# Skipped gather rows and a new place for three pieces of work in the expert stream of a two-block network

## The chip, the cores and the metric

The kernel runs on one core of a Trainium2 chip. The metric is the device time of one execution in microseconds (us). The kernel before takes 3088.03 us, the median of 3 runs (3087.74 to 3088.43).

In this text TensorE (PE) does matrix products, and PEld is its loading of stationary operands; VectorE (DVE) and ScalarE (ACT) do elementwise work, GpSimd (POOL) some elementwise work and the indirect transfers, and SyncE (SP) issues the plain DMA transfers.

## The reference, cut to what matters

The reference applies one block of attention and gated delta-rule layers and then a second block of two layers, each with a mixer, a mixture of experts and a gate. The change concerns the mixture of experts alone, which comes twice. 512 tokens of width 1024 each choose 2 of 32 experts; an expert is a gated product of width 512:

```python
def expert_block(args):
    idx, e = args
    xb = x_pad[idx]
    hb = jax.nn.silu(xb @ w_gate[e]) * (xb @ w_up[e])
    return hb @ w_down[e]
```

All inputs are float32. The two results of a token are weighted by the router's softmax and added to the residual.

## The kernel before, in words

**Routing (`route`, from L1330).** For each layer TensorE computes the router's logits, and VectorE finds the two experts of each token and the rank of each token within its expert. A one-hot product on TensorE then gives `mps`, for each slot of each expert (64 slots per expert) the number of its entry plus one, and zero where the slot is empty. `tokens` (L1470) turns this into token numbers for the gather, an empty slot becoming token 0, and `slots` (L1477) into destinations for the scatter, an empty slot becoming a number far out of range, which the scatter's bounds check leaves out. `rows` (L1483) writes the normalized tokens to a table in HBM through two SBUF buffers `xg`. Tokens beyond 64 for one expert would go through a loop of extra passes (`overflow`); in the traced execution it makes no pass.

**Gather (`gather`, L1504).** One indirect DMA on POOL brings 128 rows of 4 KB, the slots of a pair of experts, into `xg`. Later TensorE transposes them (L1519, 8 products), ScalarE and VectorE split the result into a high and a low float32r part `pk` (L425, L426), and ScalarE copies the last quarter unsplit into `xf` (L1525). The high and low part of 64 tokens stand side by side as one stationary operand of 128 columns.

**Expert stream (`experts`, L1716).** The weights of an expert come as six tiles of 1 MB. They are used in 11 units, named `(e, k, part)`: gate (k = 0, 1), up (k = 2, 3) and down (k = 4, 5). For each unit ScalarE makes the high part of a weight slice (L425, tile `wh` or `X`) and VectorE the low part by subtraction (L426, `wl` or `X`). TensorE multiplies both with `pk` (`inner`, L1562; `outer` for the down product, L1588). To save splitting work, one slice in eight of gate and up, and a quarter of down, is not split: it is multiplied as plain float32 (`also`, L1570 with `xf`, L1599 in the down product). The splits run 6 units ahead of the products (`AHEAD`), and the code of a step stands in the order split, products, further work. `pin` fixes this order on TensorE, VectorE and ScalarE: each engine executes its instructions as they are written.

The further work of a step, in the kernel before:

- at `(e, 0, 1)` `middle(e - 1)` (L1573): TensorE folds the two halves of gate and up of the expert before (L1580), ScalarE takes `tanh` (L1583), VectorE multiplies twice (L1584, L1585, tile `mth`), and ScalarE and VectorE split the result into `hk`;
- at `(e, 1, 1)` and `(e, 3, 1)` ScalarE copies the finished gate or up accumulator to SBUF (L1752), which frees it;
- at `(e, 2, 1)` of every odd expert but the last the transposes and the `pk` split of the next pair;
- after the down products `finish` (L1603) adds the halves (L1609, L1610) and scatters the rows (L1611).

There are three accumulators `acc`, taken in the order gate, up, and the two halves of the down product of the expert before. So the gate of an expert takes the buffer of the up product of the expert before it. The weight tiles have six buffers, `wh`, `wl` and `X` four each.

Of the kernel before, what the change touches and what calls it, by code (L numbers as in the profile page):

```python
# [13 lines left out]
I32 = mybir.dt.int32  # L14
# [3 lines left out]
OP = mybir.AluOpType  # L18
AX = mybir.AxisListType

P = 128
D = 1024
# [12 lines left out]
N_EXP, D_EXP = 32, 512  # L35
BLK = 64
# [143 lines left out]
class Net:  # L180
# [1142 lines left out]
    def route(self, i):  # L1323

        nc, a = self.nc, self.a
        v, act, pe = nc.vector, nc.scalar, nc.tensor
        X, rstd, gx = self.x_in
        ps = self.acc()[:72]
# [11 lines left out]
        table = self.rows(i, gx, rstd)  # L1340
# [41 lines left out]
        for c in range(NC):  # L1382
# [4 lines left out]
                               op0=OP.add, op1=OP.mult)  # L1387
# [16 lines left out]
        mps = self.aux()[:, 0:32]  # L1404
        for k in range(2):
# [3 lines left out]
            for c in range(NC):  # L1409
                pe.matmul(mps, R[:, c].rearrange("p b s -> p (b s)"), idk[:, k, c], start=(k + c == 0),  # L1410
                          stop=(k == 1 and c == NC - 1))
        tk = self.t([P, N_EXP // 2], "tk", 1, I32)
        tk2 = self.t([P, N_EXP], "tk2", 1, I32)
        self.tokens(tk2, mps)
        for b in range(2):
            v.tensor_copy(tk[b * BLK:(b + 1) * BLK], tk2[b * BLK:(b + 1) * BLK, b::2])
        mp = self.t([BLK, N_EXP], "mp", 1, I32)
        self.slots(mp, mps[:BLK])

        def weights():  # L1420

# [22 lines left out]
        def further():  # L1444
# [20 lines left out]
            v.tensor_copy(more[:, 0:1], nst[:, 31:32])  # L1465
            v.tensor_scalar(more[:, 1:], bx, float(N_EXP - 1), None, op0=OP.min)
            return place, more
        return table, tk, mp, further, weights

    def tokens(self, tk, ps):  # L1470

        v = self.nc.vector
        v.tensor_scalar(tk, ps, -1.0, 0.0, op0=OP.add, op1=OP.max)
        v.tensor_scalar(tk, tk, 1, None, op0=OP.logical_shift_right)

    def slots(self, mp, ps):

        v = self.nc.vector
        em = self.t([BLK, N_EXP], "em", 1)[:, :ps.shape[1]]
        v.tensor_scalar(em, ps, 0.0, float(1 << 20), op0=OP.is_equal, op1=OP.mult)  # L1480
        v.scalar_tensor_tensor(mp, ps, -1.0, em, op0=OP.add, op1=OP.add)

# [18 lines left out]
            self.nc.tensor.transpose(tp[:, j * P:(j + 1) * P], x(j)[:, c * P:(c + 1) * P], self.ident)  # L1501
        return tp

    def gather(self, table, idx, m):  # L1504

        nc = self.nc
        v, act, pe = nc.vector, nc.scalar, nc.tensor
        xg = self.t([P, D], "xg", 2)
        nc.gpsimd.indirect_dma_start(out=xg[:m], out_offset=None, in_=table[:, :],  # L1509
                                     in_offset=bass.IndirectOffsetOnAxis(ap=idx, axis=0),  # L1510
                                     bounds_check=S - 1, oob_is_err=False)
        yield
        n = m // BLK
        pk = self.t([P, KT, n, P], "pk", 2, FR)
        xf = self.t([P, n, BLK], "xf", 2)
        for half in range(2):
            tp = self.aux()
            for k in range(4):
                pe.transpose(tp[:, k * m:(k + 1) * m], xg[:m, (4 * half + k) * P:(4 * half + k + 1) * P],  # L1519
                             self.ident[:m, :m])  # L1520
            tv = tp[:, 0:4 * m].rearrange("p (k e t) -> p k e t", k=4, e=n)
            o = pk[:, 4 * half:4 * half + 4]
            self.split(o[:, :, :, 0:BLK], o[:, :, :, BLK:P], tv)
            if half:
                act.activation(xf, tv[:, 3], AF.Copy)  # L1525
        yield [(pk[:, :, e], xf[:, e]) for e in range(n)]
# [36 lines left out]
    def inner(self, ps, x, k, h, l, also):  # L1563

        pe = self.nc.tensor
        pk, xf = x
        for q in range(h.shape[1]):
            pe.matmul(ps, pk[:, k + q], h[:, q], start=(k + q == 0), stop=False)  # L1568
            if also is not None:
                pe.matmul(ps[0:BLK], xf, also, start=False, stop=False, skip_group_check=True)  # L1570
            pe.matmul(ps, pk[:, k + q], l[:, q], start=False, stop=also is not None)  # L1571

    def middle(self, gu):  # L1573

# [55 lines left out]
    def moe(self, i, xs, nxt):  # L1630
        nc, a = self.nc, self.a
        v, act, pe = nc.vector, nc.scalar, nc.tensor
        self.compute = [nc.tensor.engine, nc.vector.engine, nc.scalar.engine]
        ym = self.dram.tile([N_SLOT, D], F32, name=f"ym{i}", tag=f"ym{i}", bufs=1)
        table, tk, mp, further, weights = self.route(i)
        pair = lambda q: self.gather(table, tk[:, q:q + 1], P)
        g = pair(0)
        next(g)
        place, more = further()
# [8 lines left out]
        with self.tc.For_i(0, extra, 1) as b:  # L1648
            eo = nc.sync.value_load(more[0:1, bass.ds(b + 1, 1)], min_val=0, max_val=N_EXP - 1)
            sl = self.t([P, BLK], "sl", 1)  # L1650
            v.tensor_scalar(sl, self.slot1, cb, None, op0=OP.add)
            v.tensor_scalar(cb, cb, float(BLK), None, op0=OP.add)
            bc = lambda x: x.unsqueeze(1).to_broadcast([P, NC, BLK])
            mps = self.aux()[:BLK, 0:1]
            for k in range(2):
                sk = self.t([P, S], "bc", 3).rearrange("p (c s) -> p c s", c=2 * NC)[:, 0:NC]
                v.tensor_tensor(sk, place[:, k * NC:(k + 1) * NC].unsqueeze(2).to_broadcast([P, NC, BLK]), bc(sl),
                                op=OP.is_equal)
                for c in range(NC):
                    pe.matmul(mps, sk[:, c], self.ids[:, k * NC + c:k * NC + c + 1], start=(k + c == 0),  # L1660
                              stop=(k == 1 and c == NC - 1))
            mc, tc = self.t([BLK, 1], "mc", 1, I32), self.t([BLK, 1], "tc", 1, I32)
            self.slots(mc, mps)
            self.tokens(tc, mps)
            go = self.gather(table, tc, BLK)
            next(go)
            self.overflow(i, eo, next(go)[0], mc, ym)
        self.tc.no_sync_barrier()
# [45 lines left out]
    def experts(self, i, ws, xs2, pair, mp, ym, weights):  # L1714
# [3 lines left out]
        nc = self.nc  # L1718
# [10 lines left out]
        for n in range(len(units) + AHEAD):  # L1729
# [13 lines left out]
            if k < 4:  # L1743
                if (k, part) == (0, 0) and e % 2 == 0 and e + 2 < N_EXP:
                    g = pair(e // 2 + 1)
                    next(g)
                if (k % 2, part) == (0, 0):
                    acc[e] = self.acc()
                self.inner(acc[e], xs2[e // 2][e % 2], 4 * (k % 2) + 2 * part, *ready.popleft())
                if (k % 2, part) == (1, 1):  # L1750
                    gu.setdefault(e, []).append(self.tmp())
                    act.activation(gu[e][-1], acc[e], AF.Copy)  # L1752
                if (k, part) == (0, 1) and e:
                    hid[e - 1] = self.middle(gu.pop(e - 1))
                if (k, part) == (2, 1) and e % 2 and e + 1 < N_EXP:
                    xs2.append(next(g))
                if (e, k, part) == (2, 2, 0):
                    wt = weights()
            else:
                r = k % 2 * 2 + part  # L1760
                if e == N_EXP - 1 and r == 0:
                    hid[e] = self.middle(gu.pop(e))
                if r == 0:
                    acc[e, "y"] = [self.acc() for _ in range(2)]
                self.outer(acc[e, "y"], hid[e], r, *ready.popleft())
                if r == 2:
                    self.apart(self.finish(acc.pop((e, "y")), self.tmp, mp[:, e:e + 1], ym), e)
# [177 lines left out]
```

## Time and profile before

| | |
|---|---|
| median of 3 runs | 3088.03 us |
| the profiled execution | 3087.97 us |
| its span | 3086.2 us |
| TensorE busy, whole span | 2896.1 us (94%) |
| weight loads (PEld) | 2175.4 us (70%) |
| VectorE busy | 2466.1 us (80%) |
| ScalarE busy | 1755.4 us (57%) |
| GpSimd busy | 467.6 us (15%) |
| bytes moved by DMA | 599.29 MB |

The two expert streams are where the DMA engines are busiest: the page's 40 slices show 395 to 413 GB/s there, and below 160 GB/s in nearly all of the first half of the span. The first stream lies at about 1592 to 2124 us, the second at about 2447 to 2980 us. In a timeline row the columns are the start in us, the duration in us, the engine, the line, the operation, the tile written and those read, the shapes, and the number of instructions merged into the row; idle time of the engine before it, and what ended it, stand in brackets. Since instructions of one engine overlap by about 0.1 us, the time that one takes from its queue is the distance to the next start.

### The profile page before, as it was taken

How to read it: one execution, taken by the hardware profiler on the slowest of the kernel's cores; microseconds unless marked ns; L12 is line 12 of the kernel's file. 1: busy time of each engine (PE TensorE's matmuls, PEld its weight loads, DVE VectorE, ACT ScalarE, POOL GpSimd, SP SyncE). 2: the span in 40 equal slices, each digit the busy share in tenths (PEclk: the TensorE clock that was granted, in tenths of full speed). 3: DMA queues.
4: the chain of work that ended last, by engine and by line, in shares of the span. 5: the costliest groups of instructions: out<-in, count | busy, mean ns of one | idle time of the engine just before them, and what ended most of it. 6: DMA issues, size and time to landing. Idle time of an engine off the chain costs nothing.

```text
span 3086.2 us, 39076 instructions
## 1 busy us (share of the span) xinstructions
PE 2896.1 (94%) x13517; PEld 2175.4 (70%) x13517; DVE 2466.1 (80%) x4540; ACT 1755.4 (57%) x2953; POOL 467.6 (15%) x457
## 2 busy tenths in 40 slices
PE   8998999999999999999979999999997799999997
PEld 6687878886778778878855666665775566666656
DVE  7899787867998578855558888887889588888876
ACT  3554443544444333542357777876476477877864
POOL 1111110011121010020011111111122111111112
PEclk9999999999999999999989999999999899999998
DMA  5221221242211222232249999997223399999981
GB/s 159 79 62 53 72 83 62 82 127 94 75 55 62 73 78 76 90 106 79 96 195 395 413 405 401 409 397 293 65 82 113 143 394 408 411 411 404 401 305 59
DMA packets 248663, 599.29 MB, mean 194 GB/s; under 512 B 29212, under 2 KB 159726, under 8 KB 215694
## 3 DMA queue, kind: packets, MB, share of 16 engines
q1 hardware_dynamic: 237582, 567.38, 49.0%
q0 software_dynamic: 10880, 29.37, 2.7%
q8 instruction: 108, 1.77, 0.2%
q14 instruction: 93, 0.76, 0.1%
HBM read 573.60 MB, written 31.49 MB: 196 GB/s over the span
## 4 chain that ended last, share of the span: by engine, by line
PE 39%; issue 33%; DVE 16%; POOL 7%; ACT 3%; DMA 2%; POOLq 0%; SPq 0%; ACTq 0%; DVEq 0%
PE acc L521 10%; PE acc L522 10%; PE acc L520 10%; POOL ym L1611 4%; DVE wl L426 2%; DVE tmp L953 2%; PE aux L432 1%; PE aux L1111 1%; PE aux L1106 1%; POOL xg L1509 1%; PE aux L463 1%; PE aux L843 1%; DMA xg<-xr,tk 1%; DVE sel L674 1%; PE aux L828 1%
## 5 line engine op out<-in xcount | busy, mean ns | idle before, releaser
L425 ACT ACTIVATE wh<-w 128x1024 fp32r<-128x1024 f32 (+1 forms) x592 | 577.8, 1003 | 377.7 <-PE acc L521 336.2
L426 DVE TENSOR_TENSOR wl<-w,wh 128x1024 fp32r<-128x1024 f32 (+1 forms) x592 | 672.7, 1161 | 67.0 <-ACT wh L425 61.1
L520 PE MATMUL acc<-X,wh 128*128 128x512 f32 (+1 forms) x1504 | 607.4, 404 | 18.1 <-DVE tmp L898 7.0
L521 PE MATMUL acc<-X,wh 128*128 128x512 f32 (+1 forms) x1536 | 616.5, 401 | 0.3 <-DVE X L426 0.3
L522 PE MATMUL acc<-X,wl 128*128 128x512 f32 (+1 forms) x1504 | 602.0, 401 | 5.3 <-DVE wl L426 5.3
L426 DVE TENSOR_TENSOR X<-w,X 128x1024 fp32r<-128x1024 f32 (+1 forms) x352 | 380.8, 1122 | 62.7 <-ACT X L425 62.1
L425 ACT ACTIVATE X<-w 128x1024 fp32r<-128x1024 f32 (+1 forms) x352 | 326.6, 971 | 33.4 <-DMA w<-in_w_exp_gate_dram 10.7
L520 PEld LDWEIGHTS acc<-X,wh 128*128 128x128 f32 (+1 forms) x1504 | 285.5, 190 | 81.5 <-DVE tmp L898 7.4
L521 PEld LDWEIGHTS acc<-X,wh 128*128 128x128 f32 (+1 forms) x1536 | 292.0, 190 | 58.3 <-DVE X L426 1.1
L522 PEld LDWEIGHTS acc<-X,wl 128*128 128x128 f32 (+1 forms) x1504 | 285.2, 190 | 67.0 <-DVE wl L426 8.0
L1611 POOL DMA_INDIRECT ym<-yb,mp x64 | 136.6, 2134 | 807.6 <-DVE yb L1610 807.6
L1568 PE MATMUL acc<-X,pk 128*128 128x512 f32 x448 | 185.8, 415 | 20.1 <-ACT tmp L1752 14.5
L1568 PE MATMUL acc<-wh,pk 128*128 128x512 f32 x448 | 181.5, 405 | 11.6 <-ACT tmp L1752 11.6
L1571 PE MATMUL acc<-X,pk 128*128 128x512 f32 x448 | 185.9, 415 | 0.0
L1571 PE MATMUL acc<-wl,pk 128*128 128x512 f32 x448 | 183.0, 408 | 0.0
L1570 PE MATMUL acc<-w,xf 128*64 128x512 f32 x256 | 137.5, 619 | 0.0
L1571 PEld LDWEIGHTS acc<-X,pk 128*128 128x128 f32 x448 | 86.3, 193 | 66.4 <-DVE X L426 17.9
L1571 PEld LDWEIGHTS acc<-wl,pk 128*128 128x128 f32 x448 | 84.2, 188 | 65.8 <-issue 18.7
L1580 PEld LDWEIGHTS aux<-fold,tmp 128*128 128x128 f32 x1024 | 124.7, 192 | 8.1 <-ACT tmp L1752 2.7
L479 POOL TENSOR_TENSOR tmp<-tmp,tmp 128x512 f32<-128x512 f32 x60 | 86.1, 1440 | 279.8 <-ACT tmp L472 236.2
L1580 PE MATMUL aux<-fold,tmp 128*128 128x64 f32 x1024 | 122.0, 272 | 2.5 <-ACT tmp L1752 2.5
L1599 PE MATMUL acc<-w,mth 128*64 128x512 f32 x256 | 123.8, 606 | 0.0
(558 smaller groups left out, 5364.8 us busy)
## 6 DMA issues: line engine op xcount, KB each, us to landing
w<-in_w_exp_gate_dram SPq DMA_DIRECT2D x128, 1024.0 KB, 7.9
w<-in_w_exp_up_dram SPq DMA_DIRECT2D x128, 1024.0 KB, 7.8
w<-in_w_exp_down_dram SPq DMA_DIRECT2D x128, 1024.0 KB, 8.1
w<-in_w_in_dram SPq DMA_DIRECT2D x72, 1024.0 KB, 5.0
w<-in_w_in_a_dram SPq DMA_DIRECT2D x12, 1024.0 KB, 4.9
w<-in_w_out_dram SPq DMA_DIRECT2D x8, 1024.0 KB, 4.9
w<-in_w_ple_gate_dram SPq DMA_DIRECT2D x8, 1024.0 KB, 12.0
X<-ym SPq DMA_DIRECT2D x16, 512.0 KB, 5.6
```

Source lines behind the costliest of these rows:

```text
L425: self.nc.scalar.activation(h, x, AF.Copy)
L426: self.nc.vector.tensor_sub(l, x, h.bitcast(F32))
L479: nc.gpsimd.tensor_add(t, tot[0], sq)
L520: mm(ps, wh[:, k], xh[k], start=(k == 0), stop=False)
L521: mm(ps, wh[:, k], xl[k], start=False, stop=False)
L522: mm(ps, wl[:, k], xh[k], start=False, stop=(k == kt - 1))
L1568: pe.matmul(ps, pk[:, k + q], h[:, q], start=(k + q == 0), stop=False)
L1570: pe.matmul(ps[0:BLK], xf, also, start=False, stop=False, skip_group_check=True)
L1571: pe.matmul(ps, pk[:, k + q], l[:, q], start=False, stop=also is not None)
L1580: pe.matmul(fp[:, (4 * q + f) * BLK:(4 * q + f + 1) * BLK], gu[q][:, f * P:(f + 1) * P], self.fold, start=True, stop=True)
L1599: pe.matmul(pss[c][0:BLK], hv[:, 3], also[:, c], start=False, stop=False, skip_group_check=True)
L1611: return nc.gpsimd.indirect_dma_start(out=ym[:, :], out_offset=bass.IndirectOffsetOnAxis(ap=mp, axis=0), in_=y, in_offset=None, bounds_che ...
```

## The change: what it does

1. Empty slots are left out of the gather. `tokens` now shifts the scatter's numbers right by one, so an empty slot's token number is far out of range too, and the bounds check of the indirect DMA leaves its row out. Since such rows keep what was in the buffer, the two buffers `xg` are now taken once per layer and set to zero by POOL before the first gather.
2. In `inner` the unsplit product stands last in its unit, behind the products with the high and with the low part; before, it stood between them.
3. `middle(e - 1)` moves from `(e, 0, 1)` to `(e, 1, 1)`, and the transposes of the next pair from `(e, 2, 1)` to `(e, 3, 1)`. Both stand right behind the unit's products and ahead of the copy of the accumulator.

The core of the diff:

```diff
+        mp = self.t([P, N_EXP], "mp", 1, I32)
         tk2 = self.t([P, N_EXP], "tk2", 1, I32)
-        self.tokens(tk2, mps)
+        self.slots(mp, mps)
+        self.tokens(tk2, mp)
...
-        mp = self.t([BLK, N_EXP], "mp", 1, I32)
-        self.slots(mp, mps[:BLK])
...
+    def tokens(self, tk, mp):
+        self.nc.vector.tensor_scalar(tk, mp, 1, None, op0=OP.logical_shift_right)
...
-    def tokens(self, tk, ps):
-        v = self.nc.vector
-        v.tensor_scalar(tk, ps, -1.0, 0.0, op0=OP.add, op1=OP.max)
-        v.tensor_scalar(tk, tk, 1, None, op0=OP.logical_shift_right)
...
             pe.matmul(ps, pk[:, k + q], h[:, q], start=(k + q == 0), stop=False)
-            if also is not None:
-                pe.matmul(ps[0:BLK], xf, also, start=False, stop=False, skip_group_check=True)
             pe.matmul(ps, pk[:, k + q], l[:, q], start=False, stop=also is not None)
+        if also is not None:
+            pe.matmul(ps[0:BLK], xf, also, start=False, stop=True, skip_group_check=True)
...
-        pair = lambda q: self.gather(table, tk[:, q:q + 1], P)
+        xg = [self.t([P, D], "xg", 2) for _ in range(2)]
+        for x in xg:
+            nc.gpsimd.memset(x, 0.0)
+        pair = lambda q: self.gather(table, tk[:, q:q + 1], P, xg[q % 2])
...
+                if (k, part) == (1, 1) and e:
+                    hid[e - 1] = self.middle(gu.pop(e - 1))
+                if (k, part) == (3, 1) and e % 2 and e + 1 < N_EXP:
+                    xs2.append(next(g))
                 if (k % 2, part) == (1, 1):
                     gu.setdefault(e, []).append(self.tmp())
                     act.activation(gu[e][-1], acc[e], AF.Copy)
-                if (k, part) == (0, 1) and e:
-                    hid[e - 1] = self.middle(gu.pop(e - 1))
-                if (k, part) == (2, 1) and e % 2 and e + 1 < N_EXP:
-                    xs2.append(next(g))
```

The first place is ScalarE's queue around `hk` and the gate copy of an odd expert in the first stream. `wh` and `X` of 128x1024 are whole weight splits, those of 128x512 half ones; `mth` is the `tanh`, `hk` ScalarE's half of the hidden split, and the row `tmp<-acc` is the gate copy. Before:

```order
L425 ACTIVATE wh_16271<-w_16260 128x512
L1583 ACTIVATE mth_16288<-aux_16279 128x256
L425 ACTIVATE hk_16292<-mth_16288 128x4x64
L425 ACTIVATE wh_16297<-w_16295 128x1024
L425 ACTIVATE wh_16305<-w_16295 128x1024
L1752 ACTIVATE tmp_16312<-acc_16266 128x512
L425 ACTIVATE X_16316<-w_16314 128x1024
```

After the change, in the same place:

```order
L425 ACTIVATE wh_16265<-w_16254 128x512
L425 ACTIVATE wh_16275<-w_16273 128x1024
L425 ACTIVATE wh_16283<-w_16273 128x1024
L1580 ACTIVATE mth_16299<-aux_16290 128x256
L425 ACTIVATE hk_16303<-mth_16299 128x4x64
L1756 ACTIVATE tmp_16306<-acc_16260 128x512
L425 ACTIVATE X_16310<-w_16308 128x1024
```

Two whole splits that stood behind `hk` now stand ahead of `tanh`, and the gate copy stands between `hk` and the next split.

The second place is the same queue a little later, around the `pk` pieces, `xf` and the up copy (again `tmp<-acc`). Before:

```order
L425 ACTIVATE pk_16333<-aux_16335 128x8x64
L425 ACTIVATE pk_16333<-aux_16342 128x8x64
L1525 ACTIVATE xf_16334<-aux_16342 128x128
L425 ACTIVATE X_16350<-w_16324 128x1024
L425 ACTIVATE X_16359<-w_16357 128x1024
L1752 ACTIVATE tmp_16365<-acc_16319 128x512
L425 ACTIVATE wh_16367<-w_16357 128x512
L425 ACTIVATE wh_16379<-w_16377 128x1024
```

After:

```order
L425 ACTIVATE X_16327<-w_16318 128x1024
L425 ACTIVATE X_16336<-w_16334 128x1024
L425 ACTIVATE pk_16342<-aux_16344 128x8x64
L425 ACTIVATE pk_16342<-aux_16351 128x8x64
L1522 ACTIVATE xf_16343<-aux_16351 128x128
L1756 ACTIVATE tmp_16359<-acc_16313 128x512
L425 ACTIVATE wh_16361<-w_16334 128x512
L425 ACTIVATE wh_16373<-w_16371 128x1024
```

The two whole splits that followed `xf` now precede the `pk` pieces, and the up copy follows `xf` at once, with the half split behind it.

The third place is POOL's queue at the start of a stream, as a difference: four table writes from `xg`, then the first gather.

```order
-L1494 DMA xr_14322<-xg_14365 128x1024
-L1509 DMA xg_14468<-xr_14322,tk_14458 128x1024
-L1647 TENSOR_LOAD rt_3195_14498
+L1492 DMA xr_14322<-xg_14365 128x1024
+L1635 MEMSET xg_14467 128x1024
+L1635 MEMSET xg_14468 128x1024
+L1506 DMA xg_14467<-xr_14322,tk_14458 128x1024
+L1647 TENSOR_LOAD rt_3196_14500
```

The two memsets stand between the last table write and the first gather.

## Rows read from the trace of the kernel before

**Rows 1.** Busy us of each engine over 200 us; then PEclk, DMA share, GB/s

```profile
1700.00:1900.00 200.00, 195.03 (x824) 124.61 (x824) 178.12 (x208) 157.63 (x223) 36.12 (x19) 1.00 1.01 407
```

**Rows 2.** Waits of TensorE, 1700 to 2100 us: total, times, longest

```profile
PE acc L1568 <- ACT tmp L1752: 10.0, 12, 1.4
```

**Rows 3.** Lines by form, 1700 to 2100 us: busy, mean ns, idle before, releasers

```profile
L426 DVE TENSOR_TENSOR wl<-w,wh 128x1024 fp32r<-128x1024 f32 x110 | 130.7, 1220 | 15.8 <-ACT wh L425 15.6
L426 DVE TENSOR_TENSOR X<-w,X 128x1024 fp32r<-128x1024 f32 x108 | 128.3, 1220 | 15.9 <-ACT X L425 15.7
L425 ACT ACTIVATE X<-w 128x1024 fp32r<-128x1024 f32 x109 | 110.4, 1049 | 3.0 <-DMA w<-in_w_exp_gate_dram 1.7 <-DMA w<-in_w_exp_up_dram 1.1
L425 ACT ACTIVATE wh<-w 128x1024 fp32r<-128x1024 f32 x109 | 110.1, 1048 | 2.6 <-DMA w<-in_w_exp_up_dram 2.3 <-DMA w<-in_w_exp_gate_dram 0.2
```

**Rows 4.** One line's instructions, L1525: count, durations, first and last start

```profile
L1525 ACT ACTIVATE xf<-aux x14: 277/277/277, 1659.5 to 2087.7; 128x128 f32<-128x128 f32 x14
```

**Rows 5.** Timeline of ScalarE over one odd expert

```profile
1781.22 0.38 ACT L1583 ACTIVATE mth<-aux 128x256 f32<-128x256 f32 x1
1783.82 0.42 ACT L425 ACTIVATE hk<-mth 128x256 fp32r<-128x256 f32 x1 [2.22 <-DVE mth L1585]
1784.14 2.00 ACT L425 ACTIVATE wh<-w 128x1024 fp32r<-128x1024 f32 x2
1786.04 0.57 ACT L1752 ACTIVATE tmp<-acc 128x512 f32<-128x512 f32 x1
1786.52 1.99 ACT L425 ACTIVATE X<-w 128x1024 fp32r<-128x1024 f32 x2
...
1791.19 0.28 ACT L1525 ACTIVATE xf<-aux 128x128 f32<-128x128 f32 x1 [1.71 <-DVE pk L426]
1791.36 1.99 ACT L425 ACTIVATE X<-w 128x1024 fp32r<-128x1024 f32 x2
...
1793.73 0.63 ACT L425 ACTIVATE wh<-w 128x512 fp32r<-128x512 f32 x1
```

**Rows 6.** Timeline of VectorE over the same expert

```profile
1784.27 0.43 DVE L426 TENSOR_TENSOR hk<-mth,hk 128x256 fp32r<-128x256 f32 x1 [0.48 <-ACT hk L425]
1785.22 2.36 DVE L426 TENSOR_TENSOR wl<-w,wh 128x1024 fp32r<-128x1024 f32 x2 [0.52 <-ACT wh L425]
1787.60 2.36 DVE L426 TENSOR_TENSOR X<-w,X 128x1024 fp32r<-128x1024 f32 x2
1789.88 1.28 DVE L426 TENSOR_TENSOR pk<-aux,pk 128x512 fp32r<-128x512 f32 x2
1792.44 2.36 DVE L426 TENSOR_TENSOR X<-w,X 128x1024 fp32r<-128x1024 f32 x2 [1.29 <-ACT X L425]
1794.72 0.69 DVE L426 TENSOR_TENSOR wl<-w,wh 128x512 fp32r<-128x512 f32 x1
```

**Rows 7.** Timeline of TensorE: one fold, and the products before an unsplit one

```profile
1778.05 1.89 PE L1580 MATMUL aux<-fold,tmp 128*128 128x64 f32 x16
...
1798.34 0.39 PE L1571 MATMUL acc<-X,pk 128*128 128x512 f32 x1
1798.57 0.40 PE L1568 MATMUL acc<-wh,pk 128*128 128x512 f32 x1
1798.90 1.07 PE L1570 MATMUL acc<-w,xf 128*64 128x512 f32 x2
```

**Rows 8.** DMA queues, 1700 to 2100 us: packets, MB, share of 16 engines

```profile
q1 hardware_dynamic: 27221, 153.22, 94.2%
q0 software_dynamic: 3360, 8.37, 6.1%
```

**Rows 9.** Start of a stream: a memset's line, the first gather, ScalarE's waits 1590-1630

```profile
L1073 POOL MEMSET ty<- 128x512 f32 x16 | 7.9, 527 | 0.0
...
1585.83 1.08 POOL L1509 DMA_INDIRECT xg<-xr,tk  x1 [3.24 <-DVE rt L1456]
...
ACT X L425 <- DMA w<-in_w_exp_gate_dram: 4.2, 3, 2.2
```

More of the change, by code (lines that the diff above doesn't have):

```diff
@@ L1467, in further @@
             return place, more
-        return table, tk, mp, further, weights
-    def tokens(self, tk, ps):
-        v = self.nc.vector
-        v.tensor_scalar(tk, ps, -1.0, 0.0, op0=OP.add, op1=OP.max)
-        v.tensor_scalar(tk, tk, 1, None, op0=OP.logical_shift_right)
+        return table, tk, mp[:BLK], further, weights
+    def tokens(self, tk, mp):
+        self.nc.vector.tensor_scalar(tk, mp, 1, None, op0=OP.logical_shift_right)
     def slots(self, mp, ps):
         v = self.nc.vector
-        em = self.t([BLK, N_EXP], "em", 1)[:, :ps.shape[1]]
+        em = self.t([P, N_EXP], "em", 1)[:ps.shape[0], :ps.shape[1]]
         v.tensor_scalar(em, ps, 0.0, float(1 << 20), op0=OP.is_equal, op1=OP.mult)
@@ L1502, in transposed, with gather @@
         return tp
-    def gather(self, table, idx, m):
+    def gather(self, table, idx, m, xg):
         nc = self.nc
         v, act, pe = nc.vector, nc.scalar, nc.tensor
-        xg = self.t([P, D], "xg", 2)
         nc.gpsimd.indirect_dma_start(out=xg[:m], out_offset=None, in_=table[:, :],
@@ L1663, in moe @@
             self.slots(mc, mps)
-            self.tokens(tc, mps)
-            go = self.gather(table, tc, BLK)
+            self.tokens(tc, mc)
+            go = self.gather(table, tc, BLK, xg[1])
             next(go)
```

## The prediction

> **What bounds the kernel now.** The diff touches the routing ahead of the two expert streams and the streams themselves, so I first read the busy time of each engine over a long stretch of a stream [rows 1]. In 200 us TensorE shows 195.03 us of matmul, VectorE 178.12, ScalarE 157.63, and the DMA engines are full (share 1.01, 407 GB/s) at a granted clock of 1.00. Three resources look bound at once, so the shares do not decide.
>
> The waits do. TensorE waits in 12 places in 400 us, 10.0 us in all, and always at the first gate product of an expert, for ScalarE's copy of the up accumulator [rows 2]: there are three accumulators, and the next gate takes the buffer that the last up product filled. I then asked what ScalarE and VectorE wait for, line by line [rows 3]. ScalarE's weight splits wait for the DMA alone, 3.0 + 2.6 us in 400; VectorE's subtractions wait for ScalarE alone, 15.8 + 15.9 us. No wait of either names a matmul. So ScalarE and VectorE form a closed loop of two in-order queues; TensorE follows it with 10.0 / 12 = 0.8 us to spare in each pair of experts, and late weights disturb the loop a little. A pair takes (2087.7 − 1659.5) / 13 = 32.94 us [rows 4].
>
> The timelines of the two queues over one expert show where the loop loses time [rows 5, 6]. Behind the two `mth` operations VectorE waits 0.48 us for ScalarE's `hk`, and behind its own half of `hk` 0.52 us more, since ScalarE's next weight split stands behind `hk` (`hk` at 1783.82, split at 1784.14, subtraction at 1785.22). Behind the two `pk` subtractions it waits 1.29 us, for `xf` and then a whole split on ScalarE. These explain nearly all of the wait for weight splits: 2 x 0.52 + 1.29 = 2.33 us a pair are 28.3 of the 31.7 us, for the 400 / 32.94 = 12.1 pairs. The other 3.4 us, 0.28 a pair, I put down to late weights.
>
> **The change part by part.**
>
> *The gate copy moves right behind `hk`.* Before, ScalarE has `hk`, split, split, gate copy, split; now `hk`, gate copy, split. A copy takes 1786.52 − 1786.04 = 0.48 us of its queue [rows 5]. VectorE stands idle at this place, so the subtraction of 1785.22 starts 0.48 us later. What the copy cost at its old place comes back: the two subtractions from 1785.22 took 2.38 us until the next began, the next two, with no copy in the way, 1789.88 − 1787.60 = 2.28 [rows 6], so 0.10. Net 0.38 us for 31 experts of each stream (the last one's middle is issued elsewhere, unchanged): 2 x 31 x 0.38 = 23.6 us.
>
> *The up copy moves right behind `xf`, for every odd expert but the last.* Before: `xf` at 1791.19, split at 1791.36, subtraction at 1792.44. Now the copy takes 1791.36 to 1791.84, and the half-size split behind it (0.63 us) ends at 1792.47, so the first subtraction starts near 1792.51, 0.07 later. It holds VectorE about 0.60 us (two half-size `pk` pieces take 1.28), to 1793.11. The whole split behind it starts some 0.53 us after the half one (a split gives its queue free 0.1 before its end: two from 1784.14 last 2.00, the next operation starts after 1.90), at 1792.37, lasts 1.05, and its subtraction cannot start before 1793.45. Together 0.07 + 0.34 = 0.41 us [rows 5, 6]. Nothing comes back, as the copy's old place delayed no subtraction (1792.44 + 2.28 = 1794.72, where the next one starts). 2 x 15 x 0.41 = 12.3 us.
>
> *Does the moved work wait for TensorE?* One fold ended at 1778.05 + 1.89 = 1779.94, and ScalarE came to its `tanh` at 1781.22, 1.28 us later [rows 5, 7]. On TensorE the fold now stands two units later: three weight slices of two products at 0.23 us, one unsplit product of 1.07 and two joins of 0.1, 2.6 us; on ScalarE `tanh` stands two whole or half splits later, 1.9 us at most. The lead shrinks to some 0.6 us and stays positive; and were it gone, ScalarE idles 2.22 us behind `tanh` in any case. The transposes move by as much on both queues. `hk` comes two subtractions later to TensorE's down products; where that is late, TensorE first spends its 0.8 us a pair.
>
> *Fewer switches on TensorE.* A plain float32 product starts 1798.90 − 1798.57 = 0.33 us after the one before, others 0.23 [rows 7]. Putting the unsplit product, the fold and the transposes in one piece saves one way in and one way out, some 0.2 us, 2 x (31 + 15) times: 18 us of TensorE time. I count nothing, since TensorE follows; its wait grows instead.
>
> *Empty rows left out.* Each stream has 32 x 64 = 2,048 slots for 512 x 2 = 1,024 entries, so half of the rows go: 2 x 1,024 rows of 4 KB, 8.4 MB, at 407 GB/s 20.6 us of full DMA engines, 0.64 us a pair. The scatter uses the same out-of-range mark already; that it saves bytes is seen in the software queue's 8.37 MB of 400 us, where 12 whole gathers of 0.52 MB leave only 2.1 MB for 24 scatters, which would be 6.3 with every row [rows 8]. The loop gets back only what late weights cost it: 3.4 us in 400, over the 1,000 us of both streams 8.5 us. At the start of a stream ScalarE waits 4.2 us for gate weights alone, while the second and third gather share the engines [rows 9]; half of each less is 1.3 us per stream, 2.6 in all.
>
> *Routing.* One small VectorE operation more stands ahead of the first gather. The second memset fills a buffer from which the last table write reads, so it waits for that write, as the gather does (POOL idle for 3.24 us before it), and stands ahead of the gather in POOL's queue. A 128x512 memset took 0.527 us, so 128x1024 is put at 1.05 [rows 9]. The first gather starts up to 1.05 us later; whether the stream does depends on first weights and the branch, so 0 to 2.1 us for both streams; I take 1.0.
>
> **Sum.** 23.6 + 12.3 − 8.5 − 2.6 + 1.0 = +25.8 us; 2 us off, because the first expert or two of a stream wait for weights anyway and their new idle time falls into that: +24. The profiled execution took 3087.97 us around its span of 3086.2, the median of the three runs is 3088.03, so no correction: 3112 us. Its own range is 3102 to 3124.
>
> **Rivals.**
>
> *The DMA engines are the bound (faster).* For it: share 1.01, hardware queue 94.2% and software queue 6.1% [rows 1, 8]. Then half the gather's 20.6 us are the gain: 3067. Against it: if weights came last, ScalarE's splits would wait for them, and they do for 5.6 us in 400 [rows 3]. The Trainium skill (Perfetto Trace Analysis, Identifying the Most-Contended Engine and Engine Utilization) would have DMA judged by bytes against 358 GB/s per core; by that rule 407 is over the top, DMA is what to relieve, and this rival holds. The trace does not bear out 358 as a limit, since it moves more.
>
> *TensorE is the bound (faster).* For it: 195.03 of 200 us [rows 1]. Then the joins' 18 us are the gain: 3070. Against it: its wait for the up copy, once in every pair [rows 2]. The same section of the Trainium skill rejects matmul busy time as a measure and asks for the share of weight loads; that is 124.61 of 200 here, which by the rule leaves TensorE room and speaks for the forecast.
>
> *The copies hide.* If half of the two copies' 36 us falls into waits that I do not see, 18 remain and the sum is 18 − 8.5 − 2.6 + 1.0 = +8: 3096; with a little more hidden, no change. Against it: VectorE is idle at exactly these two places, behind an in-order queue.
>
> *The rows are not left out.* If skipped entries cost as much as filled ones, the 8.5 and 2.6 us come back only as far as the slower loop itself hides late weights: 3112 to 3122. The scatter speaks against it.
>
> **How the numbers follow.** Forecast 0.68, rows not left out 0.04, copies half hidden 0.13 (0.08 of it no change), DMA bound 0.11, TensorE bound 0.04. A change under 0.2% (6.2 us) cannot be told from none. Faster 0.11 + 0.04 = 0.15, same 0.08, slower 0.77. The range runs from 3084, short of the faster rivals, to 3124.
>
> **What would show it.** Right: a pair at about 33.8 us; VectorE's wait behind `hk` near 1.0 us instead of 0.52; behind `pk` 1.3 us and a second one of 0.3; ScalarE no longer waiting for weights; DMA share near 0.95; TensorE's waits longer. Wrong: a pair under 32.9 us, or VectorE's waits unchanged, which would mean that the loop was not the bound.

## The result, and the profile of the changed kernel

The changed kernel took 3114.09 us (median of 6 runs, 3110.28 to 3119.37) beside 3088.23 us (6 runs, 3087.35 to 3091.78) of the kernel before: a ratio of 1.0084, 95% interval 1.0073 to 1.0095, some 26 us slower. The forecast was 3112. Each experiment below has its own ratio, to runs of the kernel before on the same chip; two experiments are compared by the difference of their ratios times 3088 us. By the intervals such a difference is uncertain by some 4 to 7 us.

The busy time of each engine over the same stretch of a stream, to be held against [rows 1]:

```profile
1700.00:1900.00 200.00, 189.92 (x807) 121.58 (x805) 173.08 (x203) 154.12 (x219) 63.57 (x18) 1.00 1.00 391
1900.00:2100.00 200.00, 192.63 (x813) 124.45 (x814) 172.73 (x202) 155.82 (x221) 60.39 (x16) 0.99 1.00 385
```

TensorE, VectorE and ScalarE all do less in the same time, so none of them has become the bound by having more to do. The DMA engines still show a share of 1.00, but move 385 to 391 GB/s instead of 407: the share alone does not say that there is headroom. POOL is the only engine with more busy time.

One line a pair gives the pace:

```profile
L1522 ACT ACTIVATE xf<-aux x14: 277/277/278, 1663.0 to 2102.1; 128x128 f32<-128x128 f32 x14
```

(2102.1 − 1663.0) / 13 = 33.78 us a pair of experts, against 32.94 [rows 4]. The waits from 1700 to 2100 us (total, times, longest) say who waits for whom, as [rows 2] did:

```profile
ACT hk L425 <- DVE mth L1582: 60.7, 24, 2.8
ACT xf L1522 <- DVE pk L426: 22.9, 11, 2.1
...
DVE wl L426 <- ACT wh L425: 21.7, 24, 1.4
...
DVE X L426 <- ACT X L425: 20.4, 23, 1.4
...
PE acc L1565 <- ACT tmp L1756: 16.0, 11, 1.6
...
ACT mth L1580 <- PE aux L1577: 4.6, 10, 1.6
...
ACT X L425 <- DMA w<-in_w_exp_down_dram: 0.7, 1, 0.7
```

ScalarE waits once in 400 us for a weight, where it lost 3.0 + 2.6 us before [rows 3]. VectorE and ScalarE wait for each other, and TensorE's wait for the up copy has grown from 10.0 to 16.0 us: it follows the loop, now with more room. New is ScalarE's wait for the fold, ahead of its `tanh` (`mth<-aux`); VectorE's operation behind that `tanh` (L1581) still has no idle time before it in these 400 us. The two queues show where the loop got longer. ScalarE around the fold and around the transposes:

```profile
1774.92 0.42 ACT L425 ACTIVATE hk<-mth 128x256 fp32r<-128x256 f32 x1 [2.59 <-DVE mth L1582]
1775.24 0.58 ACT L1756 ACTIVATE tmp<-acc 128x512 f32<-128x512 f32 x1
1775.72 2.94 ACT L425 ACTIVATE wh<-w 128x1024 fp32r<-128x1024 f32 x3
...
1798.06 0.28 ACT L1522 ACTIVATE xf<-aux 128x128 f32<-128x128 f32 x1 [2.09 <-DVE pk L426]
1798.23 0.59 ACT L1756 ACTIVATE tmp<-acc 128x512 f32<-128x512 f32 x1
1798.71 2.53 ACT L425 ACTIVATE wh<-w 128x512 fp32r<-128x512 f32 x3
```

VectorE at the same two places:

```profile
1775.37 0.43 DVE L426 TENSOR_TENSOR hk<-mth,hk 128x256 fp32r<-128x256 f32 x1 [0.48 <-ACT hk L425]
1776.80 3.50 DVE L426 TENSOR_TENSOR wl<-w,wh 128x1024 fp32r<-128x1024 f32 x3 [1.01 <-ACT wh L425]
...
1796.74 1.28 DVE L426 TENSOR_TENSOR pk<-aux,pk 128x512 fp32r<-128x512 f32 x2
1799.37 0.69 DVE L426 TENSOR_TENSOR wl<-w,wh 128x512 fp32r<-128x512 f32 x1 [1.35 <-ACT wh L425]
1800.32 2.36 DVE L426 TENSOR_TENSOR wl<-w,wh 128x1024 fp32r<-128x1024 f32 x2 [0.26 <-ACT wh L425]
```

Read them together. `hk` starts on ScalarE at 1774.92; the gate copy goes next, at 1775.24, and holds the queue to 1775.72; only then does the split come that VectorE needs, and VectorE, done with its half of `hk` at 1775.80, stands idle for 1.01 us where [rows 6] have 0.52. At the transposes VectorE waits 1.35 us for the half split and 0.26 us more for the whole one behind it; before, one wait of 1.29.

### The profile page after: what moved, and what is told of

It is laid out like the page before. It is cut to its first block, busy times and chain, and to the rows that moved or that the text cites. A ratio compares the mean times of both kernels' runs of the same rounds, so it can differ in the third digit from the quotient of the medians.

```text
span 3110.3 us, 39244 instructions
## 1 busy us (share of the span) xinstructions
PE 2898.8 (93%) x13517; PEld 2179.6 (70%) x13517; DVE 2460.5 (79%) x4538; ACT 1753.1 (56%) x2953; POOL 609.7 (20%) x461
## 3 DMA queue, kind: packets, MB, share of 16 engines
q0 software_dynamic: 10880, 20.99, 1.8%
## 4 chain that ended last, share of the span: by engine, by line
PE 49%; DVE 23%; issue 15%; ACT 5%; POOL 4%; DMA 2%; SPq 0%; ACTq 0%; POOLq 0%; DVEq 0%
PE acc L522 9%; PE acc L520 9%; PE acc L521 9%; DVE wl L426 5%; PE acc L1565 3%; POOL ym L1608 3%; PE acc L1566 3%; DVE X L426 3%; DVE tmp L953 2%; PE aux L1577 1%; PE aux L432 1%; ACT wh L425 1%; PE acc L1568 1%; PE aux L1111 1%; PE aux L1106 1%
## 5 line engine op out<-in xcount | busy, mean ns | idle before, releaser
L1608 POOL DMA_INDIRECT ym<-yb,mp x64 | 268.4, 4194 | 676.0 <-DVE yb L1607 676.0
L1565 PEld LDWEIGHTS acc<-wh,pk 128*128 128x128 f32 x448 | 85.9, 192 | 50.6 <-ACT tmp L1756 31.5
```

The lines of the kernel that those rows point to most:

```text
L1608: return nc.gpsimd.indirect_dma_start(out=ym[:, :], out_offset=bass.IndirectOffsetOnAxis(ap=mp, axis=0), in_=y, in_offset=None, bounds_che ...
```

## The experiments

Each kernel was profiled once and timed 4 to 11 times. In the diffs `-` is the changed kernel and `+` the experiment, unless said otherwise. Line numbers shift by a few between kernels.

**The copies put ahead of fold and transposes.** Everything else of the change stays.

```
+                if (k % 2, part) == (1, 1):
+                    gu.setdefault(e, []).append(self.tmp())
+                    act.activation(gu[e][-1], acc[e], AF.Copy)
                 if (k, part) == (1, 1) and e:
                     hid[e - 1] = self.middle(gu.pop(e - 1))
                 if (k, part) == (3, 1) and e % 2 and e + 1 < N_EXP:
                     xs2.append(next(g))
-                if (k % 2, part) == (1, 1):
-                    gu.setdefault(e, []).append(self.tmp())
-                    act.activation(gu[e][-1], acc[e], AF.Copy)
```

> The changed kernel with one thing moved: the copy of the finished gate or up accumulator is issued ahead of the fold's chain or the transposes of the same step, not behind them. Loop theory (ScalarE and VectorE's queues set the time): ScalarE then idles for VectorE anyway where the copy stands, so the 0.48 us behind hk and the 0.41 us behind xf go; a pair of experts at 32.4 to 32.7 us, total 3072 to 3080 us, TensorE's wait for the up copy shorter. Rival 1 (the later place of the fold and the transposes harms by itself, hk or pk coming too late for TensorE): 3105 to 3115, with new waits of TensorE for hk or pk. Rival 2 (the gather part harms, by the memsets or by the scatter, which holds POOL 4.2 us now and 2.1 before): 3100 or more.

Measured: 3072.76 us, ratio 0.9939 (0.9926 to 0.9952), a pair (2092.2 − 1668.9) / 13 = 32.56 us. Same instructions, same new places of fold and transposes; only three lines of issue order differ from the changed kernel, and 0.0145 x 3088 = 45 us go. VectorE behind `hk` and around `pk`, and TensorE's one kind of wait left in 400 us:

```profile
1761.02 2.36 DVE L426 TENSOR_TENSOR X<-w,X 128x1024 fp32r<-128x1024 f32 x2 [0.52 <-ACT X L425]
...
1765.57 1.28 DVE L426 TENSOR_TENSOR pk<-aux,pk 128x512 fp32r<-128x512 f32 x2
1767.71 0.69 DVE L426 TENSOR_TENSOR wl<-w,wh 128x512 fp32r<-128x512 f32 x1 [0.86 <-ACT wh L425]
1768.66 1.23 DVE L426 TENSOR_TENSOR wl<-w,wh 128x1024 fp32r<-128x1024 f32 x1 [0.25 <-ACT wh L425]
```

```profile
PE acc L1593 <- DVE hk L426: 7.9, 12, 1.0
```

The wait of 1.35 us is 0.86, the one behind `hk` is 0.52 again, and TensorE no longer waits for a copy of the accumulator. It now waits for `hk`, at most 1.0 us: with the loop faster, the lateness of `hk` shows. So the loss of the change sits in the copies' places behind the two handshakes. (By a handshake I mean a point at which one of the two engines hands its result to the other and waits for what comes back.)

**The gather part alone, and the moves alone.** The first is the kernel before with the routing and gather of the change and nothing moved; the second is the changed kernel with the routing and gather of before.

> The kernel before with the gather part of the change alone: empty rows left out, two buffers zeroed, no change of order in the stream. Loop theory: only late weights and the start come back, 8.5 + 2.6 - 1.0 = 10 us: 3074 to 3082, a pair near 32.7 us. DMA rival (the engines are full, so bytes are time): 20.6 us less, 3067. Rival that the gather part harms (memsets, slower scatter): 3090 or more.

> The changed kernel without its gather part: unsplit products last, fold and transposes moved, but all 128 rows gathered as before. Loop theory: the loop's 33.8 us a pair hide the 0.64 us of DMA time a pair; total 3111 to 3120, nearly that of the whole change. DMA rival (the DMA share of the changed kernel is 1.00 too, so it is still full): 20 us more than the whole change, 3130 or more. Rival that the gather part is what harms: 3090.

Measured: the gather part alone 3078.64 us, ratio 0.9964 (0.9952 to 0.9976), a pair 32.76 us; the moves alone 3117.36 us, 1.0089 (1.0076 to 1.0102), a pair 33.83. The gather part is worth 0.0036 x 3088 = 11 us in the kernel before, not the 20.6 us that its bytes take of the DMA engines. On top of the moves it is worth 0.0005, some 1.5 us, inside the intervals: a slower loop asks for its weights later, and they are no longer late with all rows either (ScalarE waits 1.0 us in 400 for them in the second kernel). With [rows 3], which show late weights in 5.6 us of 400, this speaks against the DMA as the bound of the kernel before; the last experiment, which gains 25 us with every byte still moved, rules it out.

**One move at a time.** First the transposes back at their old place behind the second block's copy position, with the middle part still ahead of the gate copy:

```
                 if (k, part) == (1, 1) and e:
                     hid[e - 1] = self.middle(gu.pop(e - 1))
-                if (k, part) == (3, 1) and e % 2 and e + 1 < N_EXP:
-                    xs2.append(next(g))
...
+                if (k, part) == (2, 1) and e % 2 and e + 1 < N_EXP:
+                    xs2.append(next(g))
```

> The changed kernel with the transposes of the next pair, and ScalarE's and VectorE's work on them, back at their old place (two units earlier, behind the unit of the up product's second slice); the fold's chain stays at its new place ahead of the gate copy. Loop theory: the 0.41 us a pair behind xf go, 2 x 15 x 0.41 = 12 us: 3098 to 3106, a pair near 33.4 us, VectorE's wait behind hk still 1.0 us. Rival (the copies' place is not what costs, the fold's late result is): 3112 to 3116, or the whole 24 us gone.

Then the middle part back, with the transposes left where the change has them:

```
-                if (k, part) == (1, 1) and e:
-                    hid[e - 1] = self.middle(gu.pop(e - 1))
...
+                if (k, part) == (0, 1) and e:
+                    hid[e - 1] = self.middle(gu.pop(e - 1))
```

> The changed kernel with the hidden layer's middle part put back into the block in which it stood before, one block ahead of the gate half's copy; the transposes stay behind the up half's last products and ahead of its copy. Theory (each copy that stands behind a ScalarE-VectorE loop costs a bubble on both engines): only the transposes' bubble is left, so the 31 times of the gate copy come back, about 23.6 us off 3114: 3087 to 3094, a pair of experts 33.0 to 33.2 us, VectorE's wait behind hk at 0.5 us again and behind the second half of the packed tokens still at 1.3. Rival (the transposes' new place, or the products' order, costs the time): 3108 to 3118, a pair at 33.7.

Measured: 3101.59 us, ratio 1.0040 (1.0027 to 1.0052), a pair 33.57, and 3091.48 us, 1.0004 (0.9995 to 1.0013), a pair (2093.2 − 1661.6) / 13 = 33.20. Each leaves exactly the other's bubble on VectorE. The first:

```profile
1757.09 2.36 DVE L426 TENSOR_TENSOR X<-w,X 128x1024 fp32r<-128x1024 f32 x2 [1.00 <-ACT X L425]
1759.37 1.28 DVE L426 TENSOR_TENSOR pk<-aux,pk 128x512 fp32r<-128x512 f32 x2
1761.94 1.23 DVE L426 TENSOR_TENSOR wl<-w,wh 128x1024 fp32r<-128x1024 f32 x1 [1.29 <-ACT wh L425]
```

and the second:

```profile
1752.64 4.75 DVE L426 TENSOR_TENSOR X<-w,X 128x1024 fp32r<-128x1024 f32 x4 [0.53 <-ACT X L425]
...
1759.58 1.28 DVE L426 TENSOR_TENSOR pk<-aux,pk 128x512 fp32r<-128x512 f32 x2
1762.21 0.69 DVE L426 TENSOR_TENSOR wl<-w,wh 128x512 fp32r<-128x512 f32 x1 [1.35 <-ACT wh L425]
```

The gate copy's place costs 0.0080 x 3088 = 24.7 us (predicted 23.6), the up copy's place 0.0044 x 3088 = 13.6 us (predicted 12.3), each give or take some 5 us.

**The unsplit product back between the split ones**, on the changed kernel (this is the order of before):

```
             pe.matmul(ps, pk[:, k + q], h[:, q], start=(k + q == 0), stop=False)
+            if also is not None:
+                pe.matmul(ps[0:BLK], xf, also, start=False, stop=False, skip_group_check=True)
             pe.matmul(ps, pk[:, k + q], l[:, q], start=False, stop=also is not None)
-        if also is not None:
-            pe.matmul(ps[0:BLK], xf, also, start=False, stop=True, skip_group_check=True)
```

> The changed kernel with the unsplit product of each block put back between the two split ones; the moves of fold and transposes and the gather stay. Theory (ScalarE's and VectorE's loop bounds, TensorE has room): nothing to be seen, 3109 to 3120, a pair at 33.8. Rival (TensorE bounds, and the switches of kind that the new order saves or adds are worth something): 18 us of TensorE time either way, 3128 to 3136, or 3092 to 3100.

Measured: 3114.62 us, ratio 1.0070 (1.0056 to 1.0084), a pair 33.79. No change that can be told, so this part of the change does nothing here. That TensorE has room does not follow from it: the ninth experiment shows that the order takes next to no time of TensorE's off or on. What shows the room is that TensorE waits 16.0 us in 400 here and 10.0 in the kernel before [rows 2], and the last experiment, which gains 25 us with TensorE's work unchanged.

**The handshake itself taken away.** The loop loses time because ScalarE's `xf` stood behind VectorE's subtraction on `pk`. `xf` needs only the transposed tokens and nothing of that subtraction; so, on top of the kernel with the copies first, `xf` is issued ahead of that subtraction:

```
-            self.split(o[:, :, :, 0:BLK], o[:, :, :, BLK:P], tv)
+            act.activation(o[:, :, :, 0:BLK], tv, AF.Copy)
             if half:
                 act.activation(xf, tv[:, 3], AF.Copy)
+            v.tensor_sub(o[:, :, :, BLK:P], tv, o[:, :, :, 0:BLK].bitcast(F32))
```

> The kernel with the accumulators' copies ahead of fold and transposes (the first experiment), and in addition ScalarE's unsplit copy of the tokens issued right behind the second packed half and ahead of VectorE's subtraction on it, so that it no longer waits for that. Theory (a handshake between ScalarE and VectorE costs what both wait in it; here 0.86 us a pair): the two engines' loop falls to about 31.4 us a pair and the weights' DMA (about 32.2 to 32.5 us a pair at the 403 to 407 GB/s of the kernel before) bounds: a pair at 32.2 to 32.5 us against 32.56, 3062 to 3072 us against 3073. Rival (VectorE's conversions of weights set the pair, whatever the order of the copies): 3072 to 3078. Rival (TensorE's waits for the hidden layer, 1.0 us in the first experiment, grow): 3078 to 3090.

Measured: 3053.69 us, ratio 0.9873 (0.9858 to 0.9888), faster than expected: a pair takes (2078.9 − 1664.1) / 13 = 31.91 us, below the 32.2 to 32.5 at which I had put the DMA. The theory on the handshake holds, the DMA's bound does not. VectorE passes from `pk` to the weights without a wait, and TensorE is busy throughout:

```profile
1760.87 1.28 DVE L1523 TENSOR_TENSOR pk<-aux,pk 128x512 fp32r<-128x512 f32 x2
1762.07 1.82 DVE L426 TENSOR_TENSOR wl<-w,wh 128x512 fp32r<-128x512 f32 x2
```

```profile
1700.00:1900.00 200.00, 199.40 (x857) 129.54 (x856) 182.28 (x215) 164.87 (x232) 57.18 (x19) 1.00 1.01 412
```

TensorE waits for another engine once in the 400 us from 1700 on, 0.6 us: here it is the bound, at 31.9 us a pair.

**The second handshake put apart.** On top of that, ScalarE's `hk` and VectorE's half of it are issued one block behind the activation:

```
-                    hid[e - 1] = self.middle(gu.pop(e - 1))
+                    mth = self.middle(gu.pop(e - 1))
+                if (k, part) == (2, 0) and e:
+                    hid[e - 1] = self.halves(mth)
```

> As the kernel with the unsplit copy ahead of the subtraction, and the hidden layer's split into halves put one block later than its activation, so that ScalarE and VectorE have a block's conversions to do between the two. Theory of the handshakes: the loop falls to about 29.5 us a pair, far below the DMA's 32.2 to 32.5, so that nothing more than DMA's bound is to be had: 3058 to 3070 us, a pair at 32.0 to 32.4, VectorE's wait behind the first multiplication 0. Rival (the second layer's products then wait for the hidden layer, some 1.6 us later than in the first experiment, 31 times): up to 50 us on top, 3090 to 3120.

Measured: 3054.16 us, ratio 0.9883 (0.9868 to 0.9898), a pair (2074.2 − 1659.3) / 13 = 31.92. The waits for `hk` and `mth` shrink; nothing comes of it, and the rival (TensorE late for `hk`) gets 1.4 us in 400:

```profile
ACT hk L425 <- DVE mth L1583: 13.6, 25, 1.1
ACT X L425 <- DMA w<-in_w_exp_gate_dram: 11.2, 17, 1.6
```

```profile
PE acc L1598 <- DVE hk L426: 1.4, 5, 0.4
```

ScalarE now waits for weights. The reason that I give is not tested: it runs ahead of TensorE, which gives buffers free no sooner (of the waits ahead of the weights' transfers, 249.3 us in 400 are for TensorE's products, 87.6 for VectorE). Slack in this loop was worth nothing here, with TensorE full.

**The products' order, with TensorE full.** The edit of the sixth experiment, on the kernel with `xf` first.

> The kernel with the unsplit copy ahead of the subtraction, the fastest so far (3053.7 us, a pair 31.91 us, TensorE busy 399.9 of 400 us and waiting 0.6 us in 400), with the unsplit product of each block put back between the two split ones. Theory (that kernel is bound by TensorE, so now the switches of kind are seen): the two joins of 0.1 us saved 2 x (31 + 15) times come back as a loss, some 18 us: 3068 to 3076, a pair near 32.5. Rival (DMA, at 412 GB/s, is its bound): no change, 3050 to 3058.

Measured: 3056.18 us, ratio 0.9895 (0.9880 to 0.9911), a pair 31.92. The expected 18 us are not there, though TensorE is as full as before (199.90 of 200 us from 1700 on) and waits for no other engine from 1700 to 2100. The timelines say why. TensorE with the unsplit product last in its block and the fold behind it:

```profile
1765.13 0.39 PE L1567 MATMUL acc<-wl,pk 128*128 128x512 f32 x1
1765.45 1.07 PE L1569 MATMUL acc<-w,xf 128*64 128x512 f32 x2
1766.45 2.00 PE L1578 MATMUL aux<-fold,tmp 128*128 128x64 f32 x16
1768.26 0.48 PE L1566 MATMUL acc<-wh,pk 128*128 128x512 f32 x1
```

and with the unsplit product between:

```profile
1775.24 0.39 PE L1566 MATMUL acc<-X,pk 128*128 128x512 f32 x1
1775.56 1.07 PE L1568 MATMUL acc<-w,xf 128*64 128x512 f32 x2
1776.56 0.50 PE L1569 MATMUL acc<-X,pk 128*128 128x512 f32 x1
1776.90 1.89 PE L1578 MATMUL aux<-fold,tmp 128*128 128x64 f32 x16
1778.60 0.48 PE L1566 MATMUL acc<-X,pk 128*128 128x512 f32 x1
```

From the last split product ahead to the first one behind, the first takes 1768.26 − 1765.13 = 3.13 us, the second 1778.60 − 1775.24 = 3.36, with one split product of 0.23 more in it: 3.13. The 0.1 us behind an unsplit product goes with it. It lengthens the product behind it (0.34 us to the fold instead of 0.23) or the fold itself (1.81 us to the next product instead of 1.70). At the transposes the timelines differ by some 0.05 us, which is 1.5 us over the 30 times; the rest of the expected 18 us is not there.

**All rows, and the old places, with `xf` first.** Three kernels that share one edit: the fastest one with the gather of before; the gather part with every product, fold and transpose at its old place; and the kernel before with nothing changed but `xf` ahead of the subtraction, two lines exchanged.

> The same fastest kernel with the rows of empty slots gathered as before (and the routing of before): 8.4 MB more, 20.4 us of full DMA engines at 412 GB/s, 0.64 us a pair. Theory (TensorE bounds, DMA is close behind): part of it is seen, since DMA already sets a share of ScalarE's waits: 3056 to 3068, ScalarE's waits for weights longer. Rival (DMA is the bound): all of it, 3071 to 3078. Rival (DMA has room): 3050 to 3056.

> The kernel before, with the rows of empty slots left out and the unsplit copy ahead of the subtraction: fold, transposes and the unsplit product stand at their old places. Theory (both engines' loop is 32.76 - 0.86 = 31.9 us a pair, TensorE's work with the old joins some 32.5): TensorE bounds, 3068 to 3078, equal to the run with only the unsplit product put back. Rival (the joins are worth nothing): 3052 to 3060.

> The kernel before with nothing changed but the order of ScalarE's unsplit copy and VectorE's subtraction. Theory: the loop falls from 32.94 to about 32.1 us a pair, and the next bounds are TensorE at about 32.5 and DMA at 31.9 + 0.64 = 32.5 or a little less: 3068 to 3078. Rival (late weights, which all rows bring, keep the loop where it was): 3080 to 3090.

Measured: 3061.55 us, 0.9913 (0.9900 to 0.9927); 3056.87 us, 0.9899 (0.9884 to 0.9914); 3063.20 us, 0.9918 (0.9903 to 0.9932). The first as expected. The second came out at its rival: beside the ninth experiment, on the same chip (0.9895), the moved work and the joins are worth nothing that can be told. From `xf` to `xf` its pair takes 32.17 us and that of the third kernel 32.10, 0.2 to 0.3 more than 31.91, which the total times do not show as a loss. The third is better than expected, as its forecast had counted TensorE's joins and the bytes of all rows against it: 25 us gained by exchanging two lines of the kernel before. In the first of them the DMA engines did this:

```profile
1700.00:1900.00 200.00, 199.55 (x858) 129.94 (x858) 181.65 (x213) 165.11 (x231) 50.37 (x19) 1.00 1.02 421
```

With all rows they move 421 GB/s, at a share that is nearly that of the changed kernel at 385. Its pair takes (2077.3 − 1662.6) / 13 = 31.90 us, no more than with the rows left out, so in the steady stream the rows are hidden. By the ratios leaving them out is worth 0.0040 (12 us) there, but the two runs stand on different chips; on the chip of this one the ninth experiment gives 0.0018 and the old places 0.0019, some 6 us, at the edge of the intervals. The first stream's pair does not show it; in the second stream a pair takes (2918.9 − 2468.6) / 14 = 32.16 us with all rows and (2915.2 − 2469.0) / 14 = 31.87 without, 4 us over its length. Where the rest lies, if there is more, I did not settle.

## Why the prediction was right, point by point

- *The bound.* ScalarE and VectorE as a loop of two in-order queues: shown. Moving three lines of issue order costs 45 us between two kernels with the same work, at the two places named; relieving the bytes gives 11 of 20.6 us, and two lines exchanged between the two queues give 25 us in the kernel before, with the bytes and TensorE's work as they were.
- *The gate copy behind `hk`, +23.6 us.* Measured 24.7; VectorE's wait there 1.01 us, as foretold.
- *The up copy behind `xf`, +12.3 us.* Measured 13.6; the waits 1.35 and 0.26 us, where 1.3 and 0.3 were named. Both moves together, from the gather part alone to the whole change: 0.0120 x 3088 = 37.1 us, predicted 35.9.
- *Empty rows, −8.5 − 2.6 us.* The sum is right, the attribution only half. Alone the gather part gives 11 us, but on top of the moves 1.5 us, and the moves alone cost 27.5 us, not 37: the time that late weights cost comes back from the slower loop itself, with the rows or without. This was the rival of the rows that are not left out (3112 to 3122), and its arithmetic fits the moves alone (3117.36). It could not be told from the forecast by the time of the changed kernel; the bytes tell it. The rows do go: the software queue moved 5.60 MB in 400 us instead of 8.37 [rows 8], and 20.99 MB in the whole execution instead of 29.37, the 8.4 MB foretold. (The argument from the scatter took 12 whole gathers in 400 us; the trace of the kernel before lists 10, which leave 3.1 MB and not 2.1 for the scatters. That is half of what every row would be, so the argument stands.) The 2.6 us at the starts no run shows by itself; ScalarE's wait for gate weights at the first start fell from 4.2 to 2.2 us.

```profile
q1 hardware_dynamic: 26459, 149.23, 95.8%
q0 software_dynamic: 3360, 5.60, 3.7%
```

- *Routing, +1.0 us.* The memset took 951 ns where 1.05 us was estimated from [rows 9]. The first gather starts 1586.90 − 1582.78 = 4.12 us behind the start of the last table write; before it was 1585.83 − 1582.06 = 3.77. So 0.35 us in the first stream, where 0.5 was taken. Before, and then after:

```profile
1582.06 0.53 POOL L1494 DMA_DIRECT2D xr<-xg  x1 [1.28 <-ACT xg L1493]
```

```profile
1582.78 0.53 POOL L1492 DMA_DIRECT2D xr<-xg  x1 [1.28 <-ACT xg L1491]
1583.97 0.95 POOL L1635 MEMSET xg<- 128x1024 f32 x1 [0.66 <-DMA xr<-xg]
1585.78 0.95 POOL L1635 MEMSET xg<- 128x1024 f32 x1 [0.86 <-DMA xr<-xg]
1586.90 1.08 POOL L1506 DMA_INDIRECT xg<-xr,tk  x1 [0.17 <-POOL xg L1635]
```

- *Does the moved work wait for TensorE? A lead of 0.6 us that stays positive.* Wrong in part: ScalarE's `tanh` came to the fold too early in 10 of the 24 experts of 400 us, 4.6 us in all and up to 1.6. It cost nothing, for the reason that the prediction held in reserve: ScalarE idles behind `tanh` anyway, and VectorE, busy with subtractions, did not wait for it once.
- *DMA share near 0.95.* Wrong. It stayed at 1.00, while the bytes a second fell from 407 to 385–391. I had taken a full share to mean that the engines could not move more; the experiments moved 421. The Trainium skill (Perfetto Trace Analysis, Identifying the Most-Contended Engine) warns that occupancy misleads for the 16 DMA engines, and that holds here. Its Engine Utilization section gives 358 GB/s per core, but also says that a core running alone may reach about 120% of it; 421 is 118%.
- *The joins, 18 us of TensorE time.* Counted as nothing, which was right, but for the wrong reason. They were not hidden: the new order saves none of them at the fold and some 0.05 us at the transposes, as the 0.1 us goes along with the unsplit product. The rival built on them (3070) could not have happened in that way.
- *TensorE follows.* Right, and by how much could have been read: 195.03 of 200 us busy [rows 1] left 2.5%, and the pace at which it is full, 31.91 us, is 3.1% under 32.94. The same page of the Trainium skill holds matmul busy time for a poor measure of how near TensorE is to its peak, and the share of weight loads for a better one. For the question here, whether TensorE has time left, it was the other way about: weight loads fill 129.54 of 200 us in the kernel in which it has none, and matmul busy time, 199.40, with no waits, was the one to read.

## What to carry to other kernels

Where two in-order engines hand work to and fro (split here, subtract there), look for the instruction that stands first behind each handshake on either queue: anything put there that the other engine does not wait for lengthens that engine's wait by about its own length, each time. Here a copy of 0.48 us cost 24.7 / 62 = 0.40 us at the one place and 13.6 / 30 = 0.45 at the other. An independent operation belongs ahead of the handshake, not behind it; here one exchange of two lines, and not the planned moves, was worth 25 us; the fastest kernel, with the copies first and the rows left out as well, takes 3053.69 us. Price two edits together, too: time that one gives back (late weights) may already be covered by what the other costs.

## What was not expected of the hardware

POOL's scatter became longer. One scatter of before and one of after, in POOL's timeline:

```profile
1781.54 2.24 POOL L1611 DMA_INDIRECT ym<-yb,mp  x1 [13.42 <-DVE yb L1610]
```

```profile
1770.37 4.52 POOL L1608 DMA_INDIRECT ym<-yb,mp  x1 [9.84 <-DVE yb L1607]
```

Both end within 0.01 us of the moment at which VectorE next falls idle: 1783.78 before, and 1774.89 after, 0.01 us behind the second `mth` operation (1774.46 + 0.42). In the changed kernel VectorE has two subtractions more to do before it idles, and the scatter is 2.3 us longer. This is no accident of two rows: of the 64 scatters of either kernel, 57 before and 56 after end within 0.015 us of the end of a second `mth` operation. The experiments tell which move does it: the mean of the 64 is 2134 ns before and 4194 ns after, 2148 ns with the middle part back and 4050 ns with the transposes back.

Why a scatter should last until VectorE idles is open. The Trainium skill (SBUF — State Buffer, Who interferes with whom) tells of a port pair that VectorE and POOL share, where the second to come is blocked and not slowed; an end at VectorE's idle is what that would look like. But the same section infers that a `tensor_tensor`, which these subtractions are, leaves the generation of descriptors alone. No run here tries the port. No loss from it shows here: POOL idles 8 to 15 us ahead of each scatter, the last ones of the first stream take 0.90 us in either kernel, and the kernel with the copies first, whose scatters are as long (4133 ns), is the faster one.

TensorE's granted clock fell from 2.4 to 1.2 GHz for some 3.4 us five times within the changed kernel's streams, as here:

```profile
2034.00:2036.00 2.00, 0.66 (x3) 0.58 (x4) 0.65 (x2) 1.48 (x4) 0.00 (x0) 1.00 1.08 393
2036.00:2039.50 3.50, 3.50 (x10) 2.73 (x9) 3.25 (x4) 3.48 (x5) 0.00 (x0) 0.51 1.03 420
```

Ahead of it TensorE had stood idle for 1.60 us, for the up copy. That alone does not explain it: TensorE waits so 11 times in these 400 us, nearly always for 1.5 to 1.6 us, and behind all of these but this one the clock stays at 2.4 GHz. The loop does not feel the low stretch: TensorE's pair around it takes 35.2 us, by the starts of the transposes, and the next 32.4, together 67.6, two ordinary pairs, and `xf` keeps its 33.78 us throughout. What it would cost where TensorE is the bound was not tried.
